# Three contiguous HBM blocks, four stores and one shared y buffer in an add + GELU kernel

## The chip, the cores and the metric

The kernel runs on one core of a Trainium2 chip. The metric is device time in microseconds, the median over executions. Four engines of the core matter here: VectorE (DVE), ScalarE (ACT), GpSimd (POOL) and SyncE (SP), whose queue issues all transfers. TensorE does nothing. The data moves on the core's 16 DMA engines.

## What is computed

```python
def setup_inputs():
    batch, dim = 1024, 4096
    ...
def reference(x, y):
    z = x + y
    return (0.5 * z * (1 + np.tanh(np.sqrt(2 / np.pi) * (z + 0.044715 * z ** 3)))).astype(np.float32)
```

x, y and the output are float32, 16.8 MB each. Every output element depends on one element of x and one of y, so the arrays may be cut in any way as long as all three are cut alike.

## The kernel before

**Layout.** Each array is seen as 128 partitions of 32768 consecutive elements (128 KB): partition p holds rows 8p to 8p + 7. One on-chip tile z, 128 x 32768, takes x, is overwritten with x + y, and then with the result. y goes through two buffers of 8192 columns, used in turn.

**Arithmetic.** The columns are worked in 16 chunks of 2048. A chunk c takes four steps:

- `add(c)` (L149): z = z + y, on DVE for the chunks named in `by_dve`, on POOL for the others;
- `mag(c)` (L154): ACT writes |z| to a buffer w in PSUM, of which there are two (`PS`);
- `gelu(c)` (L157): ACT replaces w by GELU(−|z|), in place;
- `end(c)` (L166): DVE writes max(z, 0) + w back to z. This is GELU(z), since GELU(z) = z + GELU(−z) for positive z.

`mag(c)` needs `add(c)`, and `end(c − 2)`, which frees the w buffer. The end of chunk 8 (`FIRST`) is cut in two halves.

**Transfers.** SP issues, in this order: y0, x0, y1, x1, y2, y3, then three stores. x loads have 16384 columns (64 KB for each partition; L125), y loads 8192 (32 KB; L132), the stores 16384, 10240 and 6144 (64, 40 and 24 KB; L136). The load of y2 reuses the buffer of y0 and waits for the adds of chunks 0 to 3, y3 waits for those of chunks 4 to 7. The first store waits for the first half of `end(8)`, the second for `end(12)`, the third for `end(15)`. SP works its list in order, so a waiting transfer holds all behind it.

**Order.** The order on each engine is written out by hand (`sp`, `pool`, `acts`, `dve`). DVE's list has the ends in order of chunk; the entry `a: b` of `by_dve` puts the add of chunk a ahead of the end of chunk b. `begin_early` moves the first two loads to the very beginning of the program; `wait_late` lets the program's closing steps run while the last store is still on its way, and only then waits for that store.

Of the kernel before, what the change touches and what calls it, by code (L numbers as in the profile page):

```python
# [8 lines left out]
def begin_early(nc, count):  # L9


    head, body = (b.instructions for b in nc.main_func.blocks[:2])
    SP = mybir.EngineType.SP
    moved = [i for i in body if i.engine == SP and isinstance(i, mybir.InstDMACopy)][:count]
    assert not any(i.sync_info and i.sync_info.on_wait for i in moved)
    assert all(i.regs_accessed() == ((), ()) for i in moved)
    at = next(k for k, i in enumerate(head) if i.engine == SP)
    for k, i in enumerate(moved):
        body.remove(i)
        head.insert(at + k, i)  # L20


def wait_late(nc):

    body, end = (b.instructions for b in nc.main_func.blocks[1:3])
    last = [i for i in body if isinstance(i, mybir.InstDMACopy)][-1]
    (sem,) = [u.id for u in last.sync_info.on_update]
    all_done = end[0]  # L30
    reset = next(i for i in end if isinstance(i, mybir.InstDrain) and i.is_reset_sema)
    at = end.index(reset)
    clear = end[at + 1]
    first, stop = reset.reset_range_start, reset.reset_range_stop
    assert all_done.engine == mybir.EngineType.SP and reset.engine == mybir.EngineType.Pool
    assert isinstance(clear, mybir.InstISA) and clear.engine == mybir.EngineType.Pool
    waits = all_done.sync_info.on_wait
    (its,) = [w for w in waits if w.id == sem]

    end[0] = mybir.InstDrain(  # L40
        name=all_done.name, engine=all_done.engine, debug=all_done.debug, is_reset_sema=False,
        sync_info=mybir.SyncInfo(on_wait=[w for w in waits if w.id != sem], on_update=[]),
    )
    parts = []
    for f, e in ((first, sem), (sem + 1, stop)):
        if f < e:
            nc.gpsimd.sem_clear(range(f, e))
            parts.append(nc.cur_bb.bb.instructions.pop())
    end[at + 1 : at + 2] = parts
    end.append(  # L50
        mybir.InstEventSemaphore(
            name=clear.name, engine=mybir.EngineType.Activation, debug=clear.debug,
            sync_info=mybir.SyncInfo(
                on_wait=[its],
                on_update=[
                    mybir.SyncUpdate(
                        sync_type="semaphore", id=sem, ant_name=its.ant_name,
                        update_mode="sem-sub-imm", update_value=its.wait_value,
                    )
                ],  # L60
            ),
        )
    )


@with_exitstack
def kernel(
    ctx: ExitStack,
    tc: tile.TileContext,
    x: bass.AP,  # L70
    y: bass.AP,
    out: bass.AP,
):

    nc = tc.nc
    P = nc.NUM_PARTITIONS
    fp32 = mybir.dt.float32
    act = mybir.ActivationFunctionType
    alu = mybir.AluOpType

    N, D = x.shape
    assert N % P == 0
    TOT = N // P * D  # L90
    xv, yv, ov = (a.rearrange("(p n) d -> p (n d)", p=P) for a in (x, y, out))

    YS = 8192
    CH = 2048
    PS = 2
    xloads = [16384, 16384]
    yloads = [8192, 8192, 8192, 8192]
    FIRST = 8
    stores = [16384, 10240, 6144]

    def ranges(sizes):
        ends = [sum(sizes[: i + 1]) for i in range(len(sizes))]
        assert ends[-1] == TOT
        return [(e - f, e) for e, f in zip(ends, sizes)]

    xr, yr, sr, cr = (ranges(r) for r in (xloads, yloads, stores, [CH] * (TOT // CH)))
    C = len(cr)

    by_dve = {0: 0, 2: 0, 4: 2, 6: 4, 8: 8, 12: 10}

    def over(rs, lo, hi):
        return [i for i, (a, b) in enumerate(rs) if a < hi and b > lo]

    pool_sb = ctx.enter_context(tc.tile_pool(name="xz", bufs=1))
    pool_y = ctx.enter_context(tc.tile_pool(name="y", bufs=2))
    pool_w = ctx.enter_context(
        tc.tile_pool(name="w", bufs=PS, space=bass.MemoryType.PSUM)
    )

    zt = pool_sb.tile([P, TOT], fp32, tag="z", name="z")  # L120
    yt, wt, ends = {}, {}, {}

    def load_x(i):
        a, b = xr[i]
        nc.sync.dma_start(out=zt[:, a:b], in_=xv[:, a:b])  # L125

    def load_y(i):
        a, b = yr[i]
        s, o = divmod(a, YS)
        if o == 0:  # L130
            yt[s] = pool_y.tile([P, YS], fp32, tag="y", name=f"y{s}")
        nc.sync.dma_start(out=yt[s][:, o : o + b - a], in_=yv[:, a:b])  # L132

    def store(i):
        a, b = sr[i]
        ins = nc.sync.dma_start(out=ov[:, a:b], in_=zt[:, a:b])  # L136
        if i == 0:
            tc.add_manual_dep(
                ins.ins,
                ends[FIRST].name,  # L140
                mybir.DependencyInfo(mybir.DependencyClass.Sync, mybir.DependencyReason.DATA),
                reason="the stores join the queue when the last load is nearly done",
            )

    def add(c):
        a, b = cr[c]
        s, o = divmod(a, YS)
        eng = nc.vector if c in by_dve else nc.gpsimd
        eng.tensor_add(out=zt[:, a:b], in0=zt[:, a:b], in1=yt[s][:, o : o + b - a])  # L149

    def mag(c):
        a, b = cr[c]
        wt[c] = pool_w.tile([P, CH], fp32, tag="w", name=f"w{c}")
        nc.scalar.activation(out=wt[c], in_=zt[:, a:b], func=act.Abs)  # L154

    def gelu(c):
        nc.scalar.activation(  # L157
            out=wt[c], in_=wt[c], func=act.Gelu_apprx_tanh, scale=-1.0
        )

    def end(c):
        a, b = cr[c]
        parts = 2 if c == FIRST else 1
        n = (b - a) // parts
        for o in range(0, b - a, n):
            ins = nc.vector.scalar_tensor_tensor(  # L166
                out=zt[:, a + o : a + o + n], in0=zt[:, a + o : a + o + n], scalar=0.0,
                in1=wt[c][:, o : o + n], op0=alu.max, op1=alu.add,
            )
            ends.setdefault(c, ins.ins)  # L170


    sp = [(load_y, 0), (load_x, 0), (load_y, 1), (load_x, 1), (load_y, 2), (load_y, 3)]
    sp += [(store, i) for i in range(len(stores))]
    pool = [(add, c) for c in range(C) if c not in by_dve]
    dve, acts = [], []
    for c in range(C):
        dve += [(add, k) for k in sorted(by_dve) if by_dve[k] == c] + [(end, c)]
        acts += [(mag, c), (gelu, c)]

    needs = {
        load_x: lambda i: [],
        load_y: lambda i: [
            (add, c) for c in over(cr, yr[i][0] - 2 * YS, yr[i][1] - 2 * YS)
        ],
        add: lambda c: [(load_x, i) for i in over(xr, *cr[c])]
        + [(load_y, i) for i in over(yr, *cr[c])],
        mag: lambda c: [(add, c)] + ([(end, c - PS)] if c >= PS else []),
        gelu: lambda c: [(mag, c)],
        end: lambda c: [(gelu, c)],  # L190
        store: lambda i: [(end, c) for c in over(cr, *sr[i])] + [(end, FIRST)],
    }
    queues = [sp, pool, acts, dve]
    done = set()
    with tc.manual_schedule():
        one = pool_sb.tile([P, 1], fp32, tag="one", name="one")
        nc.vector.memset(one, 0.0)  # L197
        nc.scalar.activation(out=one, in_=one, func=act.Gelu_apprx_tanh)  # L198
        while any(queues):
            moved = False  # L200
            for q in queues:
                while q and all(n in done for n in needs[q[0][0]](q[0][1])):
                    fn, arg = q.pop(0)
                    fn(arg)
                    done.add((fn, arg))
                    moved = True
                    if q is not sp:
                        break
            assert moved, [q[:1] for q in queues]

    ctx.close()
    tc.close()
    tc.compile()  # L213
    begin_early(nc, 2)
    wait_late(nc)
# [30 lines left out]
```

## Time and profile before

| | |
|---|---|
| median of 3 runs (lowest, highest) | 120.14 us (120.08, 120.14) |
| span of the profiled execution | 118.57 us |
| DVE busy | 59.8 us (50%), 24 instructions |
| ACT busy | 60.8 us (51%), 34 instructions |
| POOL busy | 55.5 us (47%), 14 instructions |
| one add: POOL mean, DVE mean | 5.56 us, 4.01 us |
| `mag`, `gelu`, `end` on 2048 columns | 1.88, 1.86, 2.28 us |

The span runs from the first instruction to the last on the core; the median is the whole execution, 1.57 us more. A busy share is an average over the whole span, and DVE, ACT and POOL do almost nothing in the first 31 us, before the first x has landed. "SPq" in a line is SP's queue; "DMA share" is the busy time of the 16 DMA engines, and a packet is counted in the window in which it starts, so that a short window can show more than 1.

### The profile page before, as it was taken

The page shows a single profiled execution, that of the slowest core. Times are in us where ns is not written, and L with a number is a line of the kernel's source. Part 1 is how long each engine was busy: PE and PEld are TensorE (multiplying, and loading weights), DVE is VectorE, ACT ScalarE, POOL GpSimd, SP SyncE. Part 2 cuts the span into 40 slices and gives each one's busy share as a digit, 9 for nine tenths or more (in the row PEclk, how much of TensorE's full clock was granted, in tenths as well). Part 3 has the DMA queues.
Part 4 walks back from the last instruction along what each step waited for, and adds up shares of the span by engine and source line. Part 5 has one row for each costly group of instructions (what it writes and reads, how often), then busy time and mean ns, then how long its engine had stood idle before and what let it go on. Part 6 is the DMA issues. An engine that isn't in the chain of part 4 may idle for free.

```text
span 118.6 us, 160 instructions
## 1 busy us (share of the span) xinstructions
DVE 59.8 (50%) x24; ACT 60.8 (51%) x34; POOL 55.5 (47%) x14
## 2 busy tenths in 40 slices
DVE  0000000000399999699994594257999457742000
ACT  5000000000067979999379705797798999940000
POOL 0000000000399999997000029999999999100000
DMA  7989888998889988988899898998899889999996
GB/s 243 464 365 696 354 354 354 663 398 354 354 387 497 531 354 354 707 354 354 354 420 464 365 520 354 531 531 354 354 531 531 354 354 442 442 442 442 398 398 265
DMA packets 1296, 50.33 MB, mean 424 GB/s; under 512 B 144, under 2 KB 144, under 8 KB 144
## 3 DMA queue, kind: packets, MB, share of 16 engines
q1 hardware_dynamic: 1296, 50.33, 98.6%
HBM read 33.55 MB, written 16.78 MB: 424 GB/s over the span
## 4 chain that ended last, share of the span: by engine, by line
DMA 48%; POOL 34%; POOLq 4%; ACT 3%; DVE 2%; issue 0%; SPq 0%; DVEq 0%
POOL z L149 34%; DMA z<-in_x_dram 26%; DMA y<-in_y_dram 21%; POOLq L213 4%; DVE z L166 2%; ACT w L154 2%; ACT w L157 2%; SPq L132 0%; POOLq L149 0%; DVEq L166 0%
## 5 line engine op out<-in xcount | busy, mean ns | idle before, releaser
L149 POOL TENSOR_TENSOR z<-z,y 128x2048 f32<-128x2048 f32 x10 | 55.3, 5563 | 45.6 <-DMA z<-in_x_dram 31.1
L154 ACT ACTIVATE w<-z 128x2048 f32<-128x2048 f32 x16 | 30.1, 1880 | 42.5 <-DVE z L149 36.0
L166 DVE SCALAR_TENSOR_TENSOR z<-z,w 128x2048 f32<-128x2048 f32 (+1 forms) x17 | 36.4, 2157 | 16.0 <-ACT w L157 16.0
L149 DVE TENSOR_TENSOR z<-z,y 128x2048 f32<-128x2048 f32 x6 | 24.0, 4009 | 30.3 <-DMA z<-in_x_dram 30.1
L157 ACT ACTIVATE w<-w 128x2048 f32<-128x2048 f32 x16 | 29.8, 1862 | 0.5
L198 ACT ACT_TABLE_LOAD x1 | 1.3, 1283 | 1.3 <-PEq L230 1.3
L197 DVE MEMSET one<- 128x1 f32 x1 | 0.1, 59 | 1.3 <-PEq L230 1.3
L198 ACT ACTIVATE one<-one 128x1 f32<-128x1 f32 x1 | 0.2, 203 | 0.0
L230 POOL MEMSET const-float32-0.0<- 128x1 f32 x1 | 0.1, 98 | 0.2 <-issue 0.2
L230 POOL MEMSET const-bfloat16-1.0<- 128x1 bf16 x1 | 0.1, 101 | 0.0
L230 POOL MEMSET const-uint8-127<- 128x1 uint8 x1 | 0.1, 101 | 0.0
L230 POOL MEMSET const-float32-1.0<- 128x1 f32 x1 | 0.1, 98 | 0.0
## 6 DMA issues: line engine op xcount, KB each, us to landing
y<-in_y_dram SPq DMA_DIRECT2D x4, 4096.0 KB, 23.7
out_dram<-z SPq DMA_DIRECT2D x1, 5120.0 KB, 14.9
out_dram<-z SPq DMA_DIRECT2D x1, 3072.0 KB, 11.0
z<-in_x_dram SPq DMA_DIRECT2D x2, 44.9
out_dram<-z SPq DMA_DIRECT2D x1, 21.6
```

What stands on the lines that cost most here:

```text
L149: eng.tensor_add(out=zt[:, a:b], in0=zt[:, a:b], in1=yt[s][:, o : o + b - a])
L154: nc.scalar.activation(out=wt[c], in_=zt[:, a:b], func=act.Abs)
L157: nc.scalar.activation(out=wt[c], in_=wt[c], func=act.Gelu_apprx_tanh, scale=-1.0)
L166: ins = nc.vector.scalar_tensor_tensor(out=zt[:, a + o : a + o + n], in0=zt[:, a + o : a + o + n], scalar=0.0, in1=wt[c][:, o : o + n], op ...
L197: nc.vector.memset(one, 0.0)
L198: nc.scalar.activation(out=one, in_=one, func=act.Gelu_apprx_tanh)
L213: tc.compile()
L230: nc = _bacc.Bacc("TRN2", target_bir_lowering=False, num_devices=1)
```

## The change

The columns are cut into three blocks of 10240, 9984 and 12544 (40, 39 and 49 KB for each partition). In HBM a block is now one unbroken stretch: block k takes 128 x n consecutive elements, of which partition p has the n from p·n on. So which elements share a partition changes, alike for x, y and out.

- One y buffer of 20224 columns (79 KB) replaces the two of 8192. y0 lies in columns 0 to 10239, y1 from 10240 on, and y2 (12544 columns) is loaded over y0 and the first 2304 columns of y1. So y2 waits for the adds of chunks 0 to 6.
- The loads are y0, x0, y1, x1, x2, y2: still six, but x2 now goes ahead of y2, and y2 alone has a wait. There are four stores, of 10240, 9984, 7168 and 5376 columns (40, 39, 28 and 21 KB).
- 17 chunks: nine of 2048 and eight of 1792. Block 0 has chunks 0 to 4, block 1 chunks 5 to 9, block 2 chunks 10 to 16.
- DVE has the adds of chunks 0, 2, 4, 5, 7, 10, 12 and 14; POOL has nine.
- The end of chunk 8 is no longer cut in two. Store 0 waits for `end(8)`, store 1 for `end(9)`, store 2 for `end(13)`, store 3 for `end(16)`.

```diff
-    xv, yv, ov = (a.rearrange("(p n) d -> p (n d)", p=P) for a in (x, y, out))
-
-    YS = 8192
-    CH = 2048
+
+    BLOCKS = [10240, 9984, 12544]
+    CHUNKS = [2048] * 9 + [1792] * 8
+    CH = max(CHUNKS)
     PS = 2
-    xloads = [16384, 16384]
-    yloads = [8192, 8192, 8192, 8192]
     FIRST = 8
-    stores = [16384, 10240, 6144]
+    stores = [10240, 9984, 7168, 5376]
...
-    by_dve = {0: 0, 2: 0, 4: 2, 6: 4, 8: 8, 12: 10}
+    yo = [0, 10240, 0]
+    YT = 20224
+
+    xf, yf, of = (t.rearrange("n d -> (n d)") for t in (x, y, out))
+
+    def rows(flat, lo, hi):
+        (k,) = [i for i, (a, b) in enumerate(br) if a <= lo and hi <= b]
+        a, b = br[k]
+        block = flat[P * a : P * b].rearrange("(p n) -> p n", p=P)
+        return block[:, lo - a : hi - a]
+
+    by_dve = {0: 0, 2: 0, 4: 2, 5: 5, 7: 5, 10: 10, 12: 10, 14: 12}
...
+    yt = pool_sb.tile([P, YT], fp32, tag="y", name="y")
...
     def load_x(i):
-        a, b = xr[i]
-        nc.sync.dma_start(out=zt[:, a:b], in_=xv[:, a:b])
+        a, b = br[i]
+        nc.sync.dma_start(out=zt[:, a:b], in_=rows(xf, a, b))
 
     def load_y(i):
-        a, b = yr[i]
-        s, o = divmod(a, YS)
-        if o == 0:
-            yt[s] = pool_y.tile([P, YS], fp32, tag="y", name=f"y{s}")
-        nc.sync.dma_start(out=yt[s][:, o : o + b - a], in_=yv[:, a:b])
+        a, b = br[i]
+        nc.sync.dma_start(out=yt[:, yo[i] : yo[i] + b - a], in_=rows(yf, a, b))
 
     def store(i):
         a, b = sr[i]
-        ins = nc.sync.dma_start(out=ov[:, a:b], in_=zt[:, a:b])
+        ins = nc.sync.dma_start(out=rows(of, a, b), in_=zt[:, a:b])
...
-    sp = [(load_y, 0), (load_x, 0), (load_y, 1), (load_x, 1), (load_y, 2), (load_y, 3)]
+    sp = [(load_y, 0), (load_x, 0), (load_y, 1), (load_x, 1), (load_x, 2), (load_y, 2)]
...
+    def freed(i):
+        lo, hi = yo[i], yo[i] + br[i][1] - br[i][0]
+        return [
+            (add, c)
+            for c in range(C)
+            if block_of(cr[c][0]) < i and y_cols(c)[0] < hi and y_cols(c)[1] > lo
+        ]
+
     needs = {
         load_x: lambda i: [],
-        load_y: lambda i: [
-            (add, c) for c in over(cr, yr[i][0] - 2 * YS, yr[i][1] - 2 * YS)
-        ],
+        load_y: freed,
```

## The prediction

> **What bounds the kernel now.** I read first the page's DMA lines, then the DMA queue's issues, then the DMA in short windows, and last the compute timeline.
>
> ```profile
> DMA  7989888998889988988899898998899889999996
> q1 hardware_dynamic: 1296, 50.33, 98.6%
> HBM read 33.55 MB, written 16.78 MB: 424 GB/s over the span
> ```
>
> The one queue holds the 16 DMA engines for 98.6% of the span, with no empty slice. DVE, ACT and POOL are each about half busy. The chain of waits, which gives POOL 34%, ends with the last DVE instruction at 107.5 and leaves out the last store, so it doesn't say what sets the end. The issues do:
>
> ```profile
> 0.00 0.38 SPq L132 DMA_DIRECT2D y<-in_y_dram  x1
> ...
> 57.94 0.33 SPq L132 DMA_DIRECT2D y<-in_y_dram  x1
> ...
> 96.34 0.34 SPq L136 DMA_DIRECT2D out_dram<-z  x1
> ...
> 107.56 0.33 SPq L136 DMA_DIRECT2D out_dram<-z  x1
> ```
>
> With the DMA view's times to landing (the loads of y from 12.0 on; the stores 21.6, 14.9 and 11.0 after issues at 77.61, 96.34 and 107.56) and the completions that the trace records, the nine transfers land at 12.01, 31.35, 41.08, 60.44, 70.14, 79.86, 99.17, 111.26 and 118.53. Is that relay free of holes? The price of a row (one partition's piece; each engine moves eight for each transfer) tells:
>
> ```profile
> 45.00:46.00 1.00, 1.00 (x1) 1.00 (x1) 1.00 (x1) 1.00 2.42 1049
> ...
> 5.00:6.00 1.00, 0.00 (x0) 0.00 (x0) 0.00 (x0) 1.00 1.21 524
> ...
> 98.00:99.00 1.00, 1.00 (x1) 1.00 (x1) 1.00 (x1) 1.00 1.52 655
> ...
> 112.00:113.00 1.00, 0.00 (x0) 0.00 (x0) 0.00 (x0) 1.00 0.91 393
> ```
>
> The last two columns are DMA share and GB/s. The first window holds sixteen 64 KB rows (1.049 MB), 2.42 us on each engine; the others hold 32, 40 and 24 KB rows. The trace's packet records have medians of 2.418, 1.213, 1.514 and 0.912 us. These lie on one line: bytes at 27.2 GB/s for each engine plus 8.5 ns a row. Eight rows give 19.34, 9.70, 12.11 and 7.30 us, and the landings differ by 19.34, 9.73, 19.36, 9.70, 9.72, 19.31, 12.09 and 7.27. So **the engines' byte rate sets the end**: first landing plus rows, with nothing between.
>
> The first transfer, issued at 0.00, shows the price of an empty queue: 12.01 − 9.70 = **2.31 us** from issue to landing besides its rows. A transfer issued within 2.31 us of the landing ahead of it therefore opens a hole. Before, the first store (77.61 against 79.86 − 2.31 = 77.55) is on that edge, the last (107.56 against 108.95) has 1.39 us.
>
> **The change, part by part.**
>
> *Bytes and rows.* 50.33 MB stay. Each engine moves 80 rows where it moved 72, and ten completion packets (9 ns in the trace) where it moved nine: 8 × 8.5 + 9 = 0.08 us, and some 0.01 for one more junction. **+0.09 us**, all of it on the path. The trace has no 39, 49, 28 or 21 KB row; the line gives 1.477, 1.853, 1.063 and 0.799 us.
>
> For one more transfer the junctions above cost at most 0.03 us (9.73 against 9.70). The Trainium skill, "DMA: Bandwidth & Descriptors", section "Anatomy of one DMA", gives a DMA issued from GpSimd a fixed cost of about 2 us; were each transfer charged that here, one more would give 122.1, but in this full queue the measured junctions say otherwise.
>
> *Rows side by side in HBM.* Before, the rows of a transfer lie 128 KB apart; afterwards each block is one stretch. No row of the trace shows the new distance. Bounds: a gain can't exceed the excess of the first sixteen rows, which took 1.21 to 2.14 us, 0.43 us above 1.213 in the mean; later rows have no excess to lose (the 384 of 64 KB: median 2.418, mean 2.420). A loss is bounded by the dearest 64 KB row, 2.479: if all were so, 2.5% of 116.9 busy us, +2.9. I take 0, since 384 reads and writes at one rate, whatever ran beside them, point to the engine's own pace.
>
> The same page, section "Latency and other measured facts", reports under "HBM row pitch at large powers of two" 207 GB/s at a 512 KiB pitch against 214 off it, and less at larger ones. If 128 KB cost that 3% too, the change would bring about 3.5 us (116.7); the line through four row sizes above shows no such loss, and no run here has shown another distance.
>
> *Landings.* From y0's, 12.01 + 8 × (1.514 − 1.213) = 14.4: x0 26.5, y1 38.4, x1 50.2, x2 65.0, y2 79.9, stores 92.0, 103.8, 112.35, 118.6. Block 0 can start at 26.5 instead of 31.35; that alone is worth nothing, as compute isn't what ends last. What remains is whether each wait releases SP 2.31 us before the landing ahead.
>
> *The load of y2* (SP waits for DVE's add 5 and POOL's add 6, as the built program's wait values, 10 on DVE and 3 on POOL, say; the four stores queue behind it). One rule from the trace is needed: a DVE add and a POOL add exclude one another.
>
> ```profile
> 44.57 2.28 DVE L149 TENSOR_TENSOR z<-z,y 128x2048 f32<-128x2048 f32 x1
> ...
> 83.00 4.98 DVE L149 TENSOR_TENSOR z<-z,y 128x2048 f32<-128x2048 f32 x1
> ...
> L149 POOL TENSOR_TENSOR z<-z,y x10: 4502/5562/6635, 31.5 to 96.8; 128x2048 f32<-128x2048 f32 x10
> ```
>
> The second DVE add began at 83.00 beside a POOL add that ended at 85.83, and ended 2.15 later. POOL's adds take 4.50 alone and about 6.6 behind a DVE add (4.39 after its end); turns alternate. At x1's landing DVE is in end 4 till 51.2 (before, this end stood at 57.8 only because an add was put ahead of it; ACT's five chunks from 29.0 end at 48.9). So POOL's add 6 runs 50.35 to 54.86, DVE's add 5 to 57.0. y2 is issued at 57.0; its deadline is 65.0 − 2.31 = 62.7. Spare: **5.7 us**.
>
> *Store 0* needs end 8. Add 8 (POOL) to 61.4, add 7 (DVE) to 63.5, end 5 to 65.7, which frees ACT's buffer for chunk 7; two chunks at 3.7 (1.88 + 1.86) end at 73.2, end 8 at **75.6**. Deadline 79.9 − 2.31 = 77.6, spare 2.0. Before there were none to spare, so undoing the split of that chunk's end costs nothing. Store 1 (end 9, 78.6) has 11 us.
>
> *Block 2, chunks of 1792.* The 1024-column ends took 1.22 against 2.28, so DVE's cost follows columns (1.04 ns each): 2.01 for 1792. ACT and POOL have one size only: between unchanged and × 0.875. I take near 0.875 (3.26 for a chunk's two ACT instructions, 3.85 for POOL behind DVE), as DVE's rows do. From y2's 79.9: add 10 to 82.0, POOL's add 11 to 85.85, add 12 to 87.7, end 10 to 89.7, which releases ACT's chunk 12. From there ACT runs five chunks without a stop: 89.7 + 5 × 3.26 + 0.1 = 106.1, plus 0.1 + 2.01: end 16 at **108.2**. The same reckoning on before, four chunks of 3.69 from 90.21, gives 107.4 against 107.53. Store 2 (end 13) goes at 98.4 against a deadline of 101.5; store 3 at 108.2 against 112.35 − 2.31 = 110.05: spares 3.1 and **1.85**. With ACT's instructions unshortened, 7 × 0.46 = 3.2 us at most, all ahead of end 16, store 3 would be late by 1.35.
>
> *The sum.* 118.57 of the profiled span + 0.09 = 118.66. The median of the runs shown, 120.14, is 1.57 above that span; with it 120.23, **120.2 us**.
>
> **The rivals.**
>
> *One turn lost (slower).* After add 12 (87.7), DVE does two ends and then add 14; POOL does add 13 and then add 15. DVE asks after 2 × 1.93 − 0.08 = 3.79 us, POOL after 3.81 to 3.85. At 2048 columns the same pair came at 44.57 and 44.61, and DVE went first. If POOL goes first, DVE stands behind it for nearly 4 us with ends 12 to 16 queued there: by the same steps end 16 is at 111.0, 0.97 us past the deadline: 121.2. It decides once the turn adds over 1.85 us to end 16. For it: a difference under 0.06 us. Against: DVE led in every such pair of the trace.
>
> *The first rows gain (faster).* If one stretch of HBM takes the 0.43 us off the first rows: 119.8. For it: they alone run above the line. Against: the latest two starters (1.90 and 1.95) took 1.214 at the old layout, so a late descriptor, not the memory, may be what they wait for.
>
> *Dearer rows (slower).* Any part of the 2.5%: 120.4 to 123.1; only the lack of such a layout in the trace speaks for it.
>
> *The wait is coarser than the ranges.* If y2 waited for all of y1 (add 9 at 67.4), the queue would stand 67.4 − 62.7 = 4.7 us: 124.9. The wait values speak against it.
>
> **How the numbers follow.** Forecast 0.62 (120.0 to 120.4 is its own range), lost turn 0.12, first rows 0.13, dearer rows 0.11, coarse wait 0.02. 0.2% is 0.24 us, about what a measurement here can tell from no change: faster 0.13, same 0.62, slower 0.25. The range goes to 119.7 for the gain and to 121.2, the middle of the lost turn; some 0.14 stays outside.
>
> **What would show it.** Right: rows of 40, 39 and 49 KB at 1.514, 1.477 and 1.853 us, a queue at 98% or more, y2 issued near 57.0, the stores near 75.6, 78.6, 98.4 and 108.2, the last landing near 118.6. A DVE add of about 5.6 us near 91.5 would be the lost turn; a y0 that lands well before 14.4 the gain at the start; a slice with an empty queue near 65, 80 or 112 would make the forecast wrong, and name the wait that did it.

## The result and the profile after

The changed kernel takes **121.69 us** (median of 5 runs, 121.51 to 122.35) against 120.14 (120.02 to 120.32): ratio 1.0137, 95% interval 1.0121 to 1.0152. It is slower by some 1.6 us; 120.2 was forecast. The profiled execution has a span of 120.24 us against 118.57.

Here are the lines of the changed kernel's page that answer to those shown of before:

```profile
DMA  7999999999999999999896997989999999899992
q1 hardware_dynamic: 1440, 50.33, 97.7%
HBM read 33.55 MB, written 16.78 MB: 419 GB/s over the span
```

The queue still has no empty slice; the last slice has fallen from 6 tenths to 2 and the share from 98.6% to 97.7%. So the queue never ran out of work, and yet something ends late. The page's DMA issues (tensor, transfers, KB, time from issue to landing) say where:

```profile
z<-in_x_dram SPq DMA_DIRECT2D x1, 6272.0 KB, 63.6
y<-in_y_dram SPq DMA_DIRECT2D x1, 6272.0 KB, 23.5
y<-in_y_dram SPq DMA_DIRECT2D x1, 5120.0 KB, 15.3
```

y0 was issued at 0.00 and lands at 15.29, where 14.42 was forecast: 0.87 us late. x2, issued at 2.26, lands at 65.87, and y2, issued at 57.88, at 81.42: 15.55 us apart where its eight rows need 14.84, another 0.71. Each of the other eight steps from landing to landing is within 0.05 us of its rows. 0.87 + 0.71 and the 0.09 of additional rows make the 1.67 us by which the last landing moved (118.53 to 120.20).

A transfer has landed when the slowest of the 16 DMA engines is done. The completions of the single engines, as the trace records them in us, for y0 and for the last store of the changed kernel:

```
y0      14.19 14.21 14.23 14.27 14.32 14.33 14.34 14.34 14.39 14.40 14.48 14.49 14.56 14.68 14.70 15.29
store 3 118.30 118.38 118.47 118.48 118.55 118.56 118.59 118.65 118.72 118.76 118.80 118.91 118.93 118.95 118.95 120.20
```

Fifteen engines are within 0.35 us of the forecast landings (14.42 and 118.6); **one is 0.6 us behind the next from the first load on and 1.25 us behind at the end**. Before, all sixteen were within 0.43 us in y0 and 0.46 at the end. Nothing evens this out: every engine moves its own eight rows of each transfer, and the last engine is 0.56 to 0.59 us behind the next at each of the first five landings. In y0 the delay is there after the first row: that of the late engine began at 2.06 and ended at 4.36, the other fifteen had ended by 3.73.

The second loss shows in windows of the changed kernel that hold exactly one row of y2 on each engine (the last two columns are DMA share and GB/s):

```profile
75.40:76.70 1.30, 0.99 (x1) 1.27 (x2) 0.00 (x0) 1.00 1.43 618
77.20:78.50 1.30, 1.14 (x1) 0.06 (x1) 0.00 (x0) 1.00 1.62 618
```

The bytes are the same, but the last row (1.62 × 1.30 = 2.11 us in the mean, 2.74 on the late engine) takes longer than the one ahead of it (1.86). POOL is idle in both windows. At 76.42, ahead of all these last rows, SP issued the first store:

```profile
76.42 0.35 SPq L145 DMA_DIRECT2D out_dram<-z  x1
```

Before, it went at 77.61 (the line covers all three stores):

```profile
77.61 30.28 SPq L136 DMA_DIRECT2D out_dram<-z  x3
```

### The profile page after: what moved, and what is told of

Read it like the earlier page. It is cut to its first block, busy times and chain, and to the rows that moved or that the text cites. A ratio compares the mean times of both kernels' runs of the same rounds, so it can differ in the third digit from the quotient of the medians.

```text
span 120.2 us, 167 instructions
## 1 busy us (share of the span) xinstructions
DVE 69.1 (57%) x26; ACT 60.9 (51%) x36; POOL 51.6 (43%) x13
## 3 DMA queue, kind: packets, MB, share of 16 engines
q1 hardware_dynamic: 1440, 50.33, 97.7%
## 4 chain that ended last, share of the span: by engine, by line
DMA 42%; ACT 19%; issue 15%; DVE 15%; SPq 0%; DVEq 0%
DMA z<-in_x_dram 22%; DMA y<-in_y_dram 20%; ACT w L168 12%; DVE z L163 9%; ACT w L172 7%; DVE z L178 6%; SPq L141 0%; DVEq L163 0%; DVEq L178 0%
## 5 line engine op out<-in xcount | busy, mean ns | idle before, releaser
L163 POOL TENSOR_TENSOR z<-z,y 128x1792 f32<-128x1792 f32 (+1 forms) x9 | 51.4, 5738 | 51.0 <-DMA z<-in_x_dram 37.6
L168 ACT ACTIVATE w<-z 128x2048 f32<-128x2048 f32 (+1 forms) x17 | 30.2, 1779 | 44.9 <-DVE z L163 41.6
L163 DVE TENSOR_TENSOR z<-z,y 128x2048 f32<-128x2048 f32 (+1 forms) x8 | 33.2, 4184 | 28.2 <-DMA z<-in_x_dram 26.1
L172 ACT ACTIVATE w<-w 128x2048 f32<-128x2048 f32 (+1 forms) x17 | 29.9, 1761 | 0.5
```

Source lines behind the costliest of these rows:

```text
L163: eng.tensor_add(out=zt[:, a:b], in0=zt[:, a:b], in1=yt[:, o:e])
L168: nc.scalar.activation(out=wt[c][:, : b - a], in_=zt[:, a:b], func=act.Abs)
L172: nc.scalar.activation(out=wt[c][:, :n], in_=wt[c][:, :n], func=act.Gelu_apprx_tanh, scale=-1.0)
```

## The experiments

Two things were to be told apart: the new layout in HBM (theory L), and the moment at which the first store joins the queue (theory J). "The turn" below is the queue's turn from loads to stores. Every run was compared with the kernel before on the same chip; the ratios are to that kernel.

**The old layout in the changed kernel.**

```diff
-        block = flat[P * a : P * b].rearrange("(p n) -> p n", p=P)
-        return block[:, lo - a : hi - a]
+        return flat.rearrange("(p n) -> p n", p=P)[:, lo:hi]
```

> The changed kernel with the rows of every transfer 128 KB apart in HBM, as they were before; sizes, order and waits stay as changed. Theory L (the new layout slows rows where the queue starts, at the first load and at the turn from loads to stores): both excesses go, y0 lands near 14.4, y2 no more than 14.9 us after x2, 120.2 us. Theory J (the stores join the queue too early for the last load, and the first load is late for its size or for the five loads queued at once): nothing changes, 121.7 us; y0 near 15.3, y2 15.5 us after x2.

This took 121.31 us, ratio 1.0097 (1.0083 to 1.0112). Each theory was half right. The late engine is gone, and y0 lands at 14.6:

```profile
y<-in_y_dram SPq DMA_DIRECT2D x1, 5120.0 KB, 14.6
```

But the last row of y2, in a window of this kernel, is dearer still:

```profile
77.00:78.30 1.30, 1.30 (x1) 0.00 (x0) 0.00 (x0) 1.00 1.99 618
```

It takes 1.99 × 1.30 = 2.59 us in the mean (2.12 to 3.10 on the sixteen engines; 1.85 to 2.39 on fifteen and 2.74 on the late one in the changed kernel), and y2 lands 15.81 us after x2. Everything computed comes earlier by what the start no longer loses, the first store too, at 75.75; and now all sixteen engines pay. So the layout has to do with the start, and the turn costs something without it.

**Contiguous blocks in the kernel before**, two of 128 rows of 64 KB, so that y's 32 KB rows lie 64 KB apart.

```diff
-    xv, yv, ov = (a.rearrange("(p n) d -> p (n d)", p=P) for a in (x, y, out))
+    HALF = TOT // 2
+    def rows(flat, lo, hi):
+        a = lo // HALF * HALF
+        block = flat[P * a : P * (a + HALF)].rearrange("(p n) -> p n", p=P)
+        return block[:, lo - a : hi - a]
```

> The kernel before with x, y and out as two contiguous blocks of 128 rows of 64 KB, so that rows lie 64 KB apart; all else as before. Theory L: some of the loss appears, 120.5 to 121.7 us, with first rows further above 1.21 us than before and one engine behind the others. Theory J: 120.1 us.

This took 120.13 us, 1.0006 (0.9992 to 1.0020); y0 lands at 12.02, with no engine behind. So another distance between rows by itself neither costs nor gains here, and x0 and x1, whose 64 KB rows now touch, cost nothing either. But no load of y, and so not the first load, has touching rows in this kernel.

**An early first store in the kernel before.**

```diff
-    FIRST = 8
+    FIRST = 7
```

> The kernel before with the first store released by the end of chunk 7 and not 8, so that it joins the queue near 70 instead of 77.6. Theory J: rows of the last load are lengthened by 0.1 to 0.9 us, 120.5 to 121.2 us. Theory L: 120.1 us.

This took 121.03 us, 1.0078 (1.0065 to 1.0092), as theory J has it. The window with the last row but one of y3, first here and then in the kernel before:

```profile
76.40:77.30 0.90, 0.90 (x1) 0.36 (x1) 0.90 (x2) 1.00 2.32 583
```

```profile
76.40:77.30 0.90, 0.90 (x1) 0.38 (x1) 0.90 (x2) 1.00 1.35 583
```

The row takes 2.09 us in the mean where it took 1.21, 1.92 or more on every engine, and y3 lands 10.63 us after y2 and not 9.72. The store was issued at 70.04, and no row between the first ones and 76.5 was lengthened by more than 0.05 us. So the loss doesn't come at the issue: it comes at the end of the loads, when a store is already queued behind them.

**A later first store in the changed kernel**: the end of chunk 9 in halves, the store after the first.

```diff
-    FIRST = 8
+    FIRST = 9
...
+        parts = 2 if c == FIRST else 1
+        n = (b - a) // parts
+        for o in range(0, b - a, n):
...
```

> The changed kernel with its first store released by the first half of the end of chunk 9, near 78.4 instead of 76.4. Theory J: the last rows of y2 lose their excess (0.72 us on the slowest engine), while engines that are ahead may stand up to 0.8 us; 121.0 to 121.4 us. Theory L: 121.7 us, y2 still 15.5 us after x2.

This took 121.02 us, 1.0074 (1.0059 to 1.0089), 0.67 us less than the changed kernel. The store goes at 78.44, and the last row of y2 costs what the others do:

```profile
75.40:76.70 1.30, 0.95 (x1) 1.27 (x2) 0.00 (x0) 1.00 1.43 618
77.20:78.50 1.30, 1.18 (x2) 0.02 (x1) 0.00 (x0) 1.00 1.43 618
```

y2 lands 14.84 us after x2. One engine is still late from the start (y0 at 15.23; the last store at 119.31, the other fifteen by 118.82).

**Both undone**: the old layout and the later store together.

> The changed kernel with both undone: rows 128 KB apart again, and the first store released by the first half of the end of chunk 9. Theory (two separate losses, the start of the first load on one engine through the layout, and the turn from loads to stores through an early store): both are gone, 120.2 to 120.4 us, y0 at 14.4 to 14.6, y2 14.85 us after x2. If the block sizes, the order of loads or the fourth store cost something of their own, 120.6 us or more.

This took 120.25 us, 1.0017 (1.0003 to 1.0032). y0's line:

```profile
y<-in_y_dram SPq DMA_DIRECT2D x1, 5120.0 KB, 14.7
```

The last landing, 118.71, is 0.18 us above before's. The 0.09 of the rows and y0's 0.24 (14.66 for 14.42; its sixteen first rows take 2.20 us in the mean, 0.69 above 1.514, where before's were 0.43 above 1.213) are 0.33, of which the later transfers gave 0.15 back. So the layout and the moment of the store make up nearly all of the loss; for the block sizes, the order and the fourth store some 0.2 us are left (0.04 to 0.38), the 0.09 of the rows among them. The two losses don't simply add up: undoing the layout alone takes 0.0040 off the ratio, the store alone 0.0063, both together 0.0120. Without the late engine the turn costs more, 0.97 us and not 0.71.

**Rows 79 KB apart**: blocks 0 and 1 share one stretch, so that y0's rows no longer touch; later store.

```diff
-        (k,) = [i for i, (a, b) in enumerate(br) if a <= lo and hi <= b]
-        a, b = br[k]
+        a, b = (0, 20224) if hi <= 20224 else (20224, TOT)
```

> The changed kernel, first store late as in the first of these runs, but blocks 0 and 1 share one stretch of HBM whose rows lie 79 KB apart, so that y0's 40 KB rows no longer touch. If the late engine at the start comes from rows that lie end to end, it is gone: y0 by 14.6, 120.3 us. If it comes from distances between rows that are no power of two, it stays: y0 near 15.2, 121.0 us.

This took 120.34 us, 1.0018 (1.0009 to 1.0026), with y0 at 14.6. A distance that is no power of two does no harm; the late engine comes with a first load whose rows touch. Rows that touch also lie closest, 40 KB apart, and no run has rows so close that don't touch, so which of the two matters isn't shown.

**Four loads queued at the start**: x2 held until the first add, contiguous blocks, later store.

```diff
+        if i == 2:
+            tc.add_manual_dep(
+                ins.ins,
+                adds[0].name,
...
```

> The changed kernel with its contiguous blocks, first store late, and the load of x2 held until the first add, so that four loads are queued at the start and not five. If the fifth load together with the layout makes one engine late, it is gone: y0 by 14.6, 120.3 us. If the layout does it alone: y0 near 15.2, 121.0 us.

This took 120.91 us, 1.0064 (1.0050 to 1.0078). The lines of y0, first of this kernel, then of the one with rows 79 KB apart:

```profile
y<-in_y_dram SPq DMA_DIRECT2D x1, 5120.0 KB, 15.3
```

```profile
y<-in_y_dram SPq DMA_DIRECT2D x1, 5120.0 KB, 14.6
```

The fifth load isn't the cause: with it held back y0 is as late.

**A contiguous first load in the kernel before**: blocks of 32, 32 and 64 KB rows.

```diff
+        if (lo, hi) == (0, 16384):
+            return flat[: P * hi].rearrange("(k p n) -> p k n", k=2, p=P)
+        a, e = (lo, hi) if hi <= 16384 else (16384, TOT)
+        block = flat[P * a : P * e].rearrange("(p n) -> p n", p=P)
...
```

> The kernel before, with x, y and out as contiguous blocks of 32, 32 and 64 KB rows, so that y0's 32 KB rows lie end to end; x0 and the first store then move each partition's 64 KB as two rows of 32 KB (16 more rows for each engine, 0.14 us). If rows end to end in the first load make one engine late, whatever their size: y0 at 12.6 to 12.9 instead of 12.0, 120.7 to 121.0 us. If it takes the 40 KB rows of the changed kernel: y0 at 12.0, 120.2 us.

This took 120.45 us, 1.0026 (1.0014 to 1.0038). y0 lands at 12.43, above the 12.00 to 12.14 of the seven other profiles with 32 KB first rows, but short of what was expected: two engines are late, by 0.15 and 0.3 us, not one by 0.7. Of the 0.37 us, 0.14 are its additional rows. In this second kernel the direction is the same, in one profile; the size is not.

**How early is too early?** Three more moments for the first store of the kernel before: ACT's last step of chunk 8 (twice), ACT's first step of chunk 8, and the whole end of chunk 8.

```diff
-                ends[FIRST].name,
+                gelus[FIRST].name,
...
-                ends[FIRST].name,
+                mags[FIRST].name,
...
-        parts = 2 if c == FIRST else 1
+        parts = 1
```

> The kernel before with the first store released by ACT's last step of chunk 8, near 76.4, 3.0 us ahead of the end of the loads instead of 1.8. If the cost of the turn grows with that lead (none at 1.8, some 0.25 on most engines at 3.0 in the changed kernel, 1.0 at 9.4): 120.2 to 120.6 us. If it is there in full as soon as the store joins before the last row begins: 121.0 us. If the layout is needed for it: 120.1 us.

> The first store of the kernel before at 76.4 once more, as its first profile was disturbed during the load of x1, long before the store: 120.1 to 120.3 us if the turn costs nothing with a lead of 3.0 us, as that profile's last rows had it; 120.4 us or more if it does.

> The kernel before with the first store released by ACT's first step of chunk 8, near 74.5, 4.8 us ahead of the end of the loads. If the cost of an early store grows from about 3 us of lead and is complete at about 3.8: 121.0 us, y3 10.6 us after y2. If it needs a much longer lead in this kernel: 120.1 us.

> The kernel before with the end of chunk 8 in one piece, so that the first store joins near 78.7, 0.4 to 0.6 us ahead of the end of the loads. By the rule of the prediction (2.31 us ahead of the landing, 77.5) the queue stands 1.1 us: 121.2 us. By the first engine of the changed kernel with the late store (0.7 us ahead, 0.11 us lost): at most 0.4 us, 120.2 to 120.5 us.

ACT's last step of chunk 8 gave 120.67 us, 1.0034 (1.0018 to 1.0050), but its profile is disturbed: rows of x1 took up to 0.27 us more between 40 and 60 us, long before the store, so that the store went only at 77.17. The turn of that profile cost nothing. Repeated, it gave 120.50 us, 1.0031 (1.0015 to 1.0047), with the first store at 76.42 and 0.19 us lost in y3, whose last row took 1.49 us in the mean and not 1.21:

```profile
77.60:78.50 0.90, 0.90 (x2) 0.90 (x1) 0.90 (x1) 1.00 1.65 583
```

The medians of both, over 12 and 11 runs, are some 0.4 us above before's, more than the turn of either profile lost.

ACT's first step of chunk 8 gave 121.22 us, 1.0090 (1.0066 to 1.0115), with the store at 74.49 and y3 10.78 us after y2:

```profile
76.40:77.30 0.90, 0.90 (x1) 0.35 (x1) 0.90 (x2) 1.00 1.96 583
78.10:79.00 0.90, 0.64 (x1) 0.87 (x2) 0.90 (x1) 1.00 1.94 583
```

Both last rows are lengthened, from 1.21 to 1.76 and 1.75 us in the mean. The whole end gave 120.45 us, 1.0033 (1.0018 to 1.0047), with the store at 78.81, landing 19.59 us after y3 instead of 19.34. That is a hole of 0.25 us on the slowest engine, not the 1.1 of the prediction's rule; with the next step, 12.19 for 12.09, it is 0.35.

The table puts the kernels in order by the lead: the time from the first store's issue to the moment at which the last load would have landed by its rows. What is lost is read from one profile each, on the slowest engine:

| kernel | lead, us | lost at the turn, us |
|---|---|---|
| before, whole end of chunk 8 | 1.2 | 0.25 (too late) |
| changed, later store (also with the old layout, 79 KB, four loads) | 2.2 | 0.0 |
| before | 2.25 | 0.0 |
| before, gelu 8, first profile | 3.5 | 0.0 |
| before, gelu 8, second profile | 3.5 | 0.19 |
| changed | 4.3 | 0.71 |
| changed, old layout | 4.3 | 0.97 |
| before, mag 8 | 5.4 | 1.06 |
| before, `FIRST` = 7 | 9.8 | 0.91 |

The order is about the same in both kernels and both layouts: nothing lost at 2.2, nothing or 0.19 us at 3.5, 0.7 to 1.1 from 4.3 on. It is a trend and no exact curve: at the same lead of 4.3 two kernels lost 0.71 and 0.97, and the longest lead didn't lose the most. No version tried beats the kernel before.

## Why the prediction was wrong

- **What bounds the kernel**: right. The engines' bytes set the end in both. The row prices drawn from one line held within a nanosecond: 1.476, 1.854, 1.062 and 0.799 us measured (medians), 1.477, 1.853, 1.063 and 0.799 forecast.
- **The added rows, +0.09**: not contradicted; with both losses undone the kernel is 0.17% (0.03 to 0.32) above the one before.
- **"I take 0" for the rows side by side in HBM**: this step failed: the term was put at nothing for a reason that doesn't cover the start. The 384 rows it argued from all ran in a full queue, where the new layout indeed costs nothing. But the start was bounded on the side of a gain alone (0.43 us); it lost 0.87. Of this 0.2 is there with the old layout as well (14.58 and 14.66 for 14.42), so it came with the longer rows or another part of the change, and 0.6 to 0.7 came with rows that touch (15.23 to 15.30 in three profiles). The gain that was weighed beside it, should 128 KB cost something in a full queue, wasn't there: at 64 KB the kernel before is the same (1.0006).
- **"Store 0 ... spare 2.0 ... undoing the split of that chunk's end costs nothing"**: this step failed as well. It took a lead for a reserve, of which more can't harm. The store went 1.2 us earlier than before while the slowest engine's loads ended later, so the lead grew from 2.25 to 4.3 us, and 0.71 us were lost. The code's own remark, that the stores join when the last load is nearly done, stood in view, and the prediction asked only for the late side.
- **The 2.31 us rule** for that late side was too strict as well. It was measured on the first transfer, on an empty queue; a store issued 1.2 us before the landing lost 0.25 and not 1.1.
- **The waits and the compute chains**: right, moved by the late start and, in block 2, by the late y2. y2 was forecast at 57.0 and issued at 57.88, the stores at 75.6, 78.6, 98.4 and 108.2 and issued at 76.42, 79.41, 99.96 and 109.72. None opened a hole.
- **The rivals**. DVE didn't lose its turn to POOL, by 0.03 us where 0.02 to 0.06 had been reckoned:

```profile
93.02 2.01 DVE L163 TENSOR_TENSOR z<-z,y 128x1792 f32<-128x1792 f32 x1
```

POOL's add started at 93.05. "Dearer rows" was the right kind of loss, but not spread over all rows as it was priced, and 0.71 us of it came from the early store and not from the layout. What set the end were two rows of one engine, its first of y0 and its last of y2, and nothing made up for them. The first rows gained nothing, and y2 waited for its own columns alone: it went at 57.88, 0.06 us after DVE's add of chunk 5 had ended.

Why one engine is late when the rows of the first load touch, and why a store that is queued early lengthens the last rows of the loads ahead of it, is not settled: the runs show when both occur and what they cost.

## What to carry to other kernels

In a kernel that the DMA engines bound, look at the single engines' completions: a transfer lands with the slowest, and here a delay of one engine at the start stayed to the end. The moment at which the first store joins a queue of loads has two sides; here 2.2 us ahead of the last load's landing was right, 1.2 too late and 4.3 too early, and after a change of chunk sizes it has to be looked at anew. A row price taken in a full queue didn't hold here for the queue's start or its turn to stores.

## What was not expected of the hardware

A store queued early on the same queue lengthened the last one or two rows of the loads ahead of it, by up to 1.06 us in all on the slowest engine, and the stores didn't win it back. With a first load whose 40 KB rows lie end to end in HBM, one engine of the sixteen finished it 0.59 and 0.71 us behind the next in two profiles (0.47 in the kernel with four loads queued, where a second one was late too), while the same layout in later loads cost nothing, and with other distances in the first (64, 79 and 128 KB) no engine was more than 0.2 us behind.
